# A two-layer diffusion step in float32: the opening reads its first scale columns in two chunks, and sums all shift columns on TensorE

## The chip, the cores and the metric

The kernel runs on one core of a Trainium2 chip. The metric is the device time of one execution in microseconds. A change of under about 0.3% (4 us) can't be told from none with a few runs of this kernel.

## The reference, cut to what matters

128 context tokens and 512 latent tokens of width 1024 go through two layers. Every layer has a mixer and a feed-forward part, each behind a normalisation that is scaled and shifted by a modulation vector, and each added to x through a gate:

```
m = silu(cond) @ w_ada[l] + b_ada[l]          # 6 parts of 1024: shift, scale, gate, shift, scale, gate
h = rms_norm(x, g) * (1 + scale) + shift
x = x + gate * mixer(h)                        # layer 0: p = h @ w_in (1024 -> 2048), pooling and short conv, w_out
x = x + gate * swiglu(rms_norm(x, g2) * (1 + scale2) + shift2)
```

There are two condition vectors, one for the context tokens and one for the latents. So each part of m is a matrix of 1024 x 2 values, and each needs 4 MB of w_ada. For the first projection of layer 0 only the scale and, later, the shift are needed at once; everything else of m comes later.

## The kernel before, in words

x is held transposed, as 8 blocks of 128 features by 640 tokens (block k is features 128k to 128k+127). Each matmul operand is split into a high and a low float32r part, and a product of a weight block with an operand block takes three matmuls (high by high, high by low, low by high), each in two halves of 320 tokens. So one output block m takes 8 steps k of 6 matmuls. The first projection (win, 16 output blocks of 128) is called pi in the profile; two output blocks come from one 1 MB tile of weights, and each is split (`Stream.split`, `pair`, line 141) by a copy on ACT (line 144) and a subtraction on DVE (line 145).

**Scale into the operand, the rest afterwards.** `prep` (line 480) multiplies block k of x by its scale column (ACT, line 485) and forms the low part (DVE, line 487). The normalisation's factor per token is applied to the product (`scaled_main`, line 521, on DVE). The shift goes through the weights on its own: `first_bias` and `first_turn` (lines 870 to 889) for output blocks 0 to 2, and two extra columns of the operand for blocks 3 and on.

**Modulation columns, two ways.** On TensorE: `ada_load` (line 762) reads a chunk of 512 columns of w_ada (four blocks) as four DMAs of 512 KB, `ada_pe` (line 298) multiplies it by silu(cond), `ada_row` (line 322) copies the result to SBUF on ACT, `ada_turn` (line 327) turns it into columns with small matmuls, and `ada_done` (line 391) adds the bias on DVE and, for scales, makes the factor 1 + scale. On DVE: `AdaDve.run` (line 357) multiplies one block's transposed weights (a "row", one DMA of 512 KB) by the silu'd condition vectors `silb`, in two instructions of line 372, one for each condition. Both kinds of DMA land in the same six buffers (tag `araw`), so a later load waits until an earlier buffer was read.

**Order of the opening.** Lines 768 to 904 stand in a manual schedule: every engine runs them in the order written. All DMAs are issued on one queue, SP's, in order. The order on SP is scale chunk 2 (4 DMAs), constants, x blocks 0 to 3, weight tile 0 (in two halves), scale chunk 3, x blocks 4 to 7, `silb`, two rows, shift chunk 0, weight tile 1, two rows, `pwr`, weight tile 2. While data are awaited, TensorE runs filler matmuls (`turn_over`, line 812). Scale chunk 2 then gives scale blocks 0 to 3; `prep` runs for these; output blocks 0 and 1 are computed for k 0 to 3; chunk 3 gives the other scale blocks, and the same follows for k 4 to 7. `silb` gets its silu on ACT at line 843, beside that. Of the shift, blocks 0 to 3 come over TensorE and blocks 4 to 7 as four rows on DVE (lines 848 to 855). Output block 2 and the norm's second half follow, then the shifts of the three first output blocks, and the splits for block 3 (`ws.split(3)`, line 893) and block 4 (`ws.split(4)`, line 903).

**After the opening.** `project` (line 556) runs output blocks 3 to 15 of pi. For each it takes the split weights, runs `ada.run` for one or two rows (line 1053), issues the 48 matmuls, and calls `mixer_in` (line 1028). For blocks 0 to 3 that is the pooling branch (`pool_branch`, line 920: copies on ACT at line 926, sums on DVE at line 933; `pool_mid`, line 939, and `pool_end`, line 956, some blocks later), for the others the convolution. Here the order within an engine is the scheduler's, near the order of the program, with a row pinned behind the DVE instruction traced before it (line 383). PSUM has three large buffers, which pi's output blocks and the four products `py` of `pool_end` take in turn: 3, 4, 5, py 0, 6, py 1, and so on. So output block 6 takes the buffer of block 4, and can't begin until block 4 has been scaled out of it (line 523 on DVE, line 528 on ACT).

Of the kernel before, what the change touches and what calls it, by code (L numbers as in the profile page):

```python
# [9 lines left out]
F32 = mybir.dt.float32  # L10
# [26 lines left out]
EARLY = 28  # L37
# [23 lines left out]
def hybrid_step(  # L61
# [9 lines left out]
    wada0,  # L71
    wada,
# [407 lines left out]
    def prep(k, dst, l, n):  # L480
        assert (l, 3 * n + 1, 4 if (l, 3 * n + 1, 4) in known and k < 4 else 8) in known
# [273 lines left out]
    with tc.tile_pool(name="pool1", bufs=1) as p1:  # L755
# [6 lines left out]
        def ada_load(ch):  # L762
            for q in range(4):
                raw = p0.tile([P, 2, 512], F32, tag="araw", bufs=6, name=f"raw_ada{ch}_{q}")
                nc.sync.dma_start(raw, wada0[(ch + 1) // 2 if ch < 3 else 2, q])
                ada_raw.append(raw)
# [4 lines left out]
            [(0, 4, 4)]  # L771
            + [(0, 8 * p, 8) for p in (2, 4, 3)]
# [5 lines left out]
        ada_load(2)  # L778
        nc.sync.dma_start(kc, konst)
        nc.sync.dma_start(x[:, 0:4, :], xT[:, 0:4, :])  # L780
        ws.load(1, cut=True)
        ada_load(3)
        nc.sync.dma_start(x[:, 4:8, :], xT[:, 4:8, :])

        nc.sync.dma_start(silb, crows[None].broadcast_to((P, 2, D)))
        ada.load()
        ada.load()
        ada_load(0)
        ws.load(2, cut=True)
        ada.load()  # L790
        ada.load()
        pwr = p0.tile([P, 512], F32, tag="pwr", name="pwr").rearrange("p (g c) -> p g c", g=4)
        nc.sync.dma_start(pwr, pw)
        ws.load(3)
        zero = p0.tile([P, 512], F32, tag="junk", name="zero")
# [21 lines left out]
        turn_over(6)  # L817
        acc = {ch: ada_acc(ch) for ch in (2, 3)}
        ada_pe(2, acc[2], range(4))
        row = ada_row(2, acc[2])  # L820
        turn_over(3)
        ada_turn(2, row)
        turn_over(14)
        for k in range(4):
            prep(k, bufA, 0, 0)
            if k == 1:
                ws.split(0, ahead=False)
        ws.split(1, ahead=False)
        for k in range(4):
            nrm.square(k)  # L830
        first_mm(0, range(4))
        ada_pe(3, acc[3], range(4))
        row = ada_row(3, acc[3])
        nrm.add_square(V)
        nrm.add_square(V)
        nrm.add_square(V)
        nrm.add_square(V)
        first_mm(1, range(2))
        ada_turn(3, row)
        first_mm(1, range(2, 4))  # L840
        for k in range(4, 8):
            prep(k, bufA, 0, 0)
        S.activation(silb, silb, AF.Silu)
# [4 lines left out]
        ada.run(1, hold=False)  # L848
        nrm.add_square(V)
        nrm.add_square(V)  # L850
        nrm.add_square(V)
        nrm.add_square(V)
        ada.run(1, hold=False)
        ws.split(2, ahead=False)
        ada.run(2, hold=False)
# [783 lines left out]
```

## Time and profile before

| | us |
|---|---|
| median of 3 runs | 1356.52 (1354.65 to 1358.49) |
| the profiled execution | 1359.17 |
| its span in the profile | 1357.0 |

The profile is of one execution. Its span runs from the first to the last instruction, and some 2.2 us of the execution's time lie around it. PE is TensorE, DVE VectorE, ACT ScalarE, SP the engine that issues the DMAs. Starts are in us from the beginning of the span. PE's granted clock is 1.00 where it runs at 2.4 GHz and 0.50 at 1.2 GHz.

### The profile page before, as it was taken

The page shows a single profiled execution, that of the slowest core. Times are in us where ns is not written, and L with a number is a line of the kernel's source. Part 1 is how long each engine was busy: PE and PEld are TensorE (multiplying, and loading weights), DVE is VectorE, ACT ScalarE, POOL GpSimd, SP SyncE. Part 2 cuts the span into 40 slices and gives each one's busy share as a digit, 9 for nine tenths or more (in the row PEclk, how much of TensorE's full clock was granted, in tenths as well). Part 3 has the DMA queues.
Part 4 walks back from the last instruction along what each step waited for, and adds up shares of the span by engine and source line. Part 5 has one row for each costly group of instructions (what it writes and reads, how often), then busy time and mean ns, then how long its engine had stood idle before and what let it go on. Part 6 is the DMA issues. An engine that isn't in the chain of part 4 may idle for free.

```text
span 1357.0 us, 22469 instructions
## 1 busy us (share of the span) xinstructions
PE 1327.6 (98%) x8952; PEld 1295.8 (95%) x8952; DVE 1076.8 (79%) x2095; ACT 638.5 (47%) x1159; POOL 46.3 (3%) x56
## 2 busy tenths in 40 slices
PE   9999999999999999999999999999999999999996
PEld 6899999999999999999998999999999999999995
DVE  4899897978999999999877677599877777446744
ACT  5433245753145521554666675477541355314543
POOL 0000000000000000000012221000000000000001
PEclk9899999999999999999999999999999999999998
DMA  9735422115433454344431110141144122311212
GB/s 366 284 109 190 168 94 94 63 63 171 171 124 111 156 189 151 124 135 161 148 101 48 48 48 32 34 154 47 47 140 164 39 94 70 118 63 63 78 47 78
DMA packets 36808, 155.54 MB, mean 115 GB/s; under 512 B 3936, under 2 KB 11104, under 8 KB 25952
## 3 DMA queue, kind: packets, MB, share of 16 engines
q1 hardware_dynamic: 36704, 154.12, 32.8%
q8 instruction: 70, 1.15, 0.3%
q14 instruction: 34, 0.28, 0.1%
HBM read 148.60 MB, written 2.88 MB: 112 GB/s over the span
## 4 chain that ended last, share of the span: by engine, by line
PE 82%; DVE 11%; ACT 3%; issue 2%; DMA 1%; SPq 0%; POOL 0%; DVEq 0%; ACTq 0%; POOLq 0%
PE fi L632 28%; PE fo L289 19%; PE fi L289 8%; PE pi L289 7%; PE pq L289 5%; PE po L289 4%; DVE junk L372 3%; PE wb L289 2%; PE wa L289 2%; PE o L1355 2%; PE s L1305 2%; DVE wl_fi_p L145 1%; PE t L1338 1%; ACT wh_fi_p L144 1%; DMA x<-xT 1%
## 5 line engine op out<-in xcount | busy, mean ns | idle before, releaser
L144 ACT ACTIVATE wh_fi_p<-raw_fi 128x512 fp32r<-128x512 f32 x252 | 154.5, 626 | 232.0 <-PE fi L632 123.6
L372 DVE CUSTOM_DVE_ANT_0 junk<-rawa,silb 128x512 f32<-128x512 f32 (+1 forms) x280 | 224.1, 800 | 5.9 <-DMA rawa<-wada 1.7
L145 DVE TENSOR_TENSOR wl_fi_p<-raw_fi,wh_fi_p 128x512 fp32r<-128x512 f32 x252 | 171.4, 687 | 65.0 <-ACT wh_fi_p L144 65.0
L144 ACT ACTIVATE wh_fo<-raw_fo 128x1024 fp32r<-128x1024 f32 (+1 forms) x48 | 47.5, 990 | 147.4 <-PE fo L289 122.8
L508 DVE SCALAR_TENSOR_TENSOR x<-fo,mod,x 128x128 f32<-128x128 f32 (+1 forms) x144 | 55.8, 434 | 70.4 <-PE fo L289 67.2
L632 PE MATMUL fi<-bh,wh_fi_p 128*128 128x320 f32 x288 | 88.8, 308 | 1.8 <-DVE x L508 1.8
L632 PE MATMUL fi<-bh,wl_fi_p 128*128 128x320 f32 x288 | 88.9, 309 | 0.0
L632 PE MATMUL fi<-ah,wl_fi_p 128*128 128x320 f32 x288 | 88.7, 308 | 0.0
L632 PE MATMUL fi<-al,wh_fi_p 128*128 128x320 f32 x288 | 88.7, 308 | 0.0
L632 PE MATMUL fi<-ah,wh_fi_p 128*128 128x320 f32 x288 | 88.5, 307 | 0.0
L632 PE MATMUL fi<-bl,wh_fi_p 128*128 128x320 f32 x288 | 88.4, 307 | 0.0
L289 PE MATMUL fo<-al,wh_fo 128*128 128x320 f32 x352 | 80.8, 310 | 0.0
L289 PE MATMUL fo<-ah,wh_fo 128*128 128x320 f32 x352 | 80.6, 310 | 0.1
L289 PE MATMUL fo<-ah,wl_fo 128*128 128x320 f32 x352 | 80.4, 309 | 0.0
L289 PE MATMUL fo<-bh,wh_fo 128*128 128x320 f32 x328 | 75.2, 310 | 0.0
L289 PE MATMUL fo<-bh,wl_fo 128*128 128x320 f32 x328 | 75.0, 310 | 0.0
L289 PE MATMUL fo<-bl,wh_fo 128*128 128x320 f32 x328 | 74.9, 310 | 0.0
L632 PE MATMUL fi<-x0h,wh_fi_p 128*128 128x320 f32 x216 | 68.1, 320 | 1.5 <-ACT fi L644 0.9
L632 PE MATMUL fi<-xh,wh_fi_p 128*128 128x320 f32 x216 | 67.9, 320 | 0.2
L632 PE MATMUL fi<-xh,wl_fi_p 128*128 128x320 f32 x216 | 66.5, 309 | 0.0
L632 PE MATMUL fi<-xl,wh_fi_p 128*128 128x320 f32 x216 | 66.5, 309 | 0.0
L632 PE MATMUL fi<-x0h,wl_fi_p 128*128 128x320 f32 x216 | 66.4, 308 | 0.0
(372 smaller groups left out, 3786.7 us busy)
## 6 DMA issues: line engine op xcount, KB each, us to landing
raw_fi<-wfi SPq DMA_DIRECT2D x44, 1024.0 KB, 4.7
rawa<-wada SPq DMA_DIRECT2D x84, 512.0 KB, 3.4
raw_fo<-wfo SPq DMA_DIRECT2D x16, 1024.0 KB, 4.9
raw_ada<-wada SPq DMA_DIRECT2D x12, 512.0 KB, 7.3
raw_in<-win SPq DMA_DIRECT2D x6, 1024.0 KB, 5.3
raw_fo<-wfo SPq DMA_DIRECT2D x8, 768.0 KB, 4.2
raw_qkv<-wqkv SPq DMA_DIRECT2D x6, 1024.0 KB, 5.4
raw_out<-wout SPq DMA_DIRECT2D x4, 1024.0 KB, 5.2
```

Source lines behind the costliest of these rows:

```text
L144: S.activation(h, src, AF.Copy)
L145: eng.tensor_tensor(out=l, in0=src, in1=h.bitcast(F32), op=ALU.subtract)
L289: PE.matmul(ps[:, h, 0 : hi - lo], w[a][:, k, cols], rhs[b][:, k0 + k, lo:hi], start=k == 0 and a == b, stop=k == kn - 1 and a == 1,)
L372: op = V.tensor_tensor_reduce(out=self.junk, in0=raw[:, cols], in1=self.silb[:, c, cols], scale=1.0, scalar=0.0, op0=ALU.mult, op1=ALU.add ...
L508: V.scalar_tensor_tensor(out=xs, in0=got[:, 0 : b - a], scalar=mod[l][:, gate0 + m, c : c + 1], in1=xs, op0=ALU.mult, op1=ALU.add,)
L632: PE.matmul(out, w[a][:, k, :], ops.get(OPERAND[p], b)[:, k, :], start=fresh and k == 0 and a == b, stop=k == ops.kn - 1 and a == 1, skip_ ...
L1305: PE.matmul(self.ps[:, hf, 0:HT], bufB[a][:, self.h, q0 : q0 + P], kt[b][:, self.kv, hf * HT : hf * HT + HT], start=n == 0, stop=n == 2,)
L1338: PE.transpose(flat(pt)[:, s * P : s * P + P], self.pe[:, s * P : s * P + P], ident)
L1355: PE.matmul(po[:, 0 : 2 * P], vt[a][:, self.kv, s * P : s * P + P], got[b][:, s, :], start=s == 0 and n == 0, stop=s == 4 and n == 2,)
```

## The change

Scale blocks 0 to 3 are read as two chunks of 256 columns (two blocks each, 1 MB in two DMAs), and x blocks 0 to 3 as two DMAs of two blocks. The new function `ada_half` sums one such chunk on TensorE, and `ada_half_turn` turns it. The first two output blocks start with k 0 and 1; the second half chunk and k 2 and 3 follow. The shift's blocks 4 to 7 become chunk 1 on TensorE, so the four early rows on DVE go. On SP weight tile 1 and both shift chunks now stand ahead of `silb`. The silu of `silb` moves to the end of the opening, between the last `first_turn` and the split for block 4, and two rows on DVE follow that split. The rows of the output blocks 3 to 15 are given by a list, 14 in all where 16 were. Output block 2's steps are spread anew between the shift's sums. The array of rows shrinks by the four blocks that are no longer rows, and the array of chunks changes accordingly. The diff leaves out a new argument, a looser assertion in `prep`, and one index of the last rows (76 becomes 72).

```diff
@@ -34,7 +34,9 @@
 PLAIN = 4
 RAW = 3
 
-EARLY = 28
+EARLY = 24
+
+PI_ROWS = (1, 0, 0, 1, 0, 1, 2, 1, 2, 1, 2, 1, 2)
...
@@ -762,36 +765,42 @@
         def ada_load(ch):
             for q in range(4):
                 raw = p0.tile([P, 2, 512], F32, tag="araw", bufs=6, name=f"raw_ada{ch}_{q}")
-                nc.sync.dma_start(raw, wada0[(ch + 1) // 2 if ch < 3 else 2, q])
+                nc.sync.dma_start(raw, wada0[min(ch, 2), q])
+                ada_raw.append(raw)
+
+        def ada_load_half(half):
+            for q in range(2):
+                raw = p0.tile([P, 4, 256], F32, tag="araw", bufs=6, name=f"raw_adah{half}_{q}")
+                nc.sync.dma_start(raw, wadah[half, q])
                 ada_raw.append(raw)
 
         startup = ExitStack()
         startup.enter_context(tc.manual_schedule())
         ada = AdaDve(
-            [(0, 4, 4)]
-            + [(0, 8 * p, 8) for p in (2, 4, 3)]
+            [(0, 8 * p, 8) for p in (2, 4, 3)]
             + [(0, 40 + b, 1) for b in range(8)]
             + [(1, 8 * p, 8) for p in (1, 0, 2, 4, 3)]
         )
         ada.home(p0, p1, 6, junk, silb)
         ada.limit = EARLY
-        ada_load(2)
+        pwr = p0.tile([P, 512], F32, tag="pwr", name="pwr").rearrange("p (g c) -> p g c", g=4)
+        ada_load_half(0)
         nc.sync.dma_start(kc, konst)
-        nc.sync.dma_start(x[:, 0:4, :], xT[:, 0:4, :])
+        nc.sync.dma_start(x[:, 0:2, :], xT[:, 0:2, :])
         ws.load(1, cut=True)
+        ada_load_half(1)
+        nc.sync.dma_start(x[:, 2:4, :], xT[:, 2:4, :])
         ada_load(3)
         nc.sync.dma_start(x[:, 4:8, :], xT[:, 4:8, :])
+        ws.load(2, cut=True)
+        ada_load(0)
+        ada_load(1)
 
         nc.sync.dma_start(silb, crows[None].broadcast_to((P, 2, D)))
-        ada.load()
-        ada.load()
-        ada_load(0)
-        ws.load(2, cut=True)
-        ada.load()
-        ada.load()
-        pwr = p0.tile([P, 512], F32, tag="pwr", name="pwr").rearrange("p (g c) -> p g c", g=4)
         nc.sync.dma_start(pwr, pw)
         ws.load(3)
+        for _ in range(4):
+            ada.load()
         zero = p0.tile([P, 512], F32, tag="junk", name="zero")
         G.memset(zero, 0.0)
         zeror2 = p0.tile([P, 512], F32R, tag="zero", name="zeror")
@@ -814,53 +823,88 @@
             for _ in range(n):
                 PE.matmul(idle, zeror, zeror2, start=True, stop=True)
 
-        turn_over(6)
-        acc = {ch: ada_acc(ch) for ch in (2, 3)}
-        ada_pe(2, acc[2], range(4))
-        row = ada_row(2, acc[2])
+        half_acc = ada_acc("h")
+
+        def ada_half(half):
+            out = half_acc[:, 256 * half : 256 * half + 256]
+            for q in range(2):
+                raw = ada_raw.pop(0)
+                for j in range(4):
+                    PE.matmul(
+                        out[32 * j : 32 * j + 2, :],
+                        silc[:, 4 * q + j, :],
+                        raw[:, j, :],
+                        start=False,
+                        stop=q == 1,
+                        tile_position=(0, 32 * j),
+                        skip_group_check=True,
+                    )
+            row = tmp(f"rowh_{half}")[0:98, 0:256]
+            S.activation(row, out[0:98, :], AF.Copy)
+            return row
+
+        def ada_half_turn(half, row):
+            ps = ps_small(f"adath_{half}")
+            for b in range(2):
+                PE.matmul(
+                    ps[:, 2 * b : 2 * b + 2],
+                    row[:, b * P : b * P + P],
+                    kc[0:98, C_SUM : C_SUM + 2],
+                    start=True,
+                    stop=True,
+                )
+            ada_done(0, 8 + 2 * half, ps[:, 0:4].rearrange("p (b c) -> p b c", c=2))
+
+        turn_over(4)
+        row = ada_half(0)
         turn_over(3)
-        ada_turn(2, row)
-        turn_over(14)
-        for k in range(4):
+        ada_half_turn(0, row)
+        turn_over(10)
+        for k in range(2):
             prep(k, bufA, 0, 0)
-            if k == 1:
+            if k == 0:
                 ws.split(0, ahead=False)
         ws.split(1, ahead=False)
+        first_mm(0, range(2))
+        row = ada_half(1)
+        first_mm(1, range(1))
+        ada_half_turn(1, row)
+        first_mm(1, range(1, 2))
+        for k in range(2, 4):
+            prep(k, bufA, 0, 0)
         for k in range(4):
             nrm.square(k)
-        first_mm(0, range(4))
-        ada_pe(3, acc[3], range(4))
-        row = ada_row(3, acc[3])
-        nrm.add_square(V)
-        nrm.add_square(V)
-        nrm.add_square(V)
-        nrm.add_square(V)
-        first_mm(1, range(2))
+        first_mm(0, range(2, 4))
+        acc = ada_acc(3)
+        ada_pe(3, acc, range(4))
+        row = ada_row(3, acc)
+        for _ in range(4):
+            nrm.add_square(V)
+        first_mm(1, range(2, 4))
         ada_turn(3, row)
-        first_mm(1, range(2, 4))
         for k in range(4, 8):
             prep(k, bufA, 0, 0)
-        S.activation(silb, silb, AF.Silu)
+        ws.split(2, ahead=False)
         for k in range(4, 8):
             nrm.square(k)
         first_mm(0, range(4, 8))
         first_mm(1, range(4, 8))
-        ada.run(1, hold=False)
-        nrm.add_square(V)
-        nrm.add_square(V)
-        nrm.add_square(V)
-        nrm.add_square(V)
-        ada.run(1, hold=False)
-        ws.split(2, ahead=False)
-        ada.run(2, hold=False)
-        S.preload_act_table_set("natural_log_exp_and_others")
+        for _ in range(4):
+            nrm.add_square(V)
+        first_mm(2, range(0, 2))
         acc = ada_acc(0)
         ada_pe(0, acc, range(4))
         row = ada_row(0, acc)
+        S.preload_act_table_set("natural_log_exp_and_others")
+        first_mm(2, range(2, 3))
+        ada_turn(0, row)
         nrm.finish((0, HT), None)
-        first_mm(2, range(0, 1))
-        ada_turn(0, row)
-        first_mm(2, range(1, 5))
+        first_mm(2, range(3, 4))
+        acc = ada_acc(1)
+        ada_pe(1, acc, range(4))
+        row = ada_row(1, acc)
+        first_mm(2, range(4, 5))
+        ada_turn(1, row)
         prep_shift(bufA, 0, 0)
         for b, t in enumerate(bufA):
             V.tensor_copy(shr[:, :, 2 * b : 2 * b + 2], t[:, :, T:TX].bitcast(F32))
@@ -888,11 +932,11 @@
             PE.matmul(pb[:, 0:2], row, kc[0:4, C_SEL : C_SEL + 2], start=True, stop=True)
             S.activation(fev[m][:, T:TX], pb[:, 0:2], AF.Copy)
 
-        first_mm(2, range(5, 6))
+        first_mm(2, range(5, 7))
         row = first_bias(0)
         ws.split(3, ahead=False)
         fev.append(scaled_main(first[1], "ev_1"))
-        first_mm(2, range(6, 8))
+        first_mm(2, range(7, 8))
         fev.append(scaled_main(first[2], "ev_2"))
         pwp = tuple(t[:, KB - 1, 0:512].rearrange("p (g c) -> p g c", g=4) for t in bufB)
         pair(pwp, pwr)
@@ -900,7 +944,9 @@
         rows = [first_bias(m) for m in (1, 2)]
         for m in (1, 2):
             first_turn(m, rows[m - 1])
+        S.activation(silb, silb, AF.Silu)
         ws.split(4, ahead=False)
+        ada.run(2, hold=False)
         startup.close()
 
 
@@ -1050,7 +1096,7 @@
             13,
             lambda i, ps: mixer_in(i + 3, scaled(ps, f"ev_{i + 3}")),
             ext=True,
-            each=lambda i: ada.run(1 + (5 <= i < 8)),
+            each=lambda i: ada.run(PI_ROWS[i]),
         )
 
...
@@ -1614,7 +1659,8 @@
         "rope": _rope(),
         "ckT": i["cache_k"][0, 0].transpose(2, 1, 0),
         "cv": i["cache_v"][0, 0],
-        "wada0": i["w_ada"][0].reshape(4, 2, P, 12, 512)[:, :, :, [0, 2, 3]].transpose(3, 0, 2, 1, 4),
+        "wada0": i["w_ada"][0].reshape(4, 2, P, 12, 512)[:, :, :, [0, 1, 3]].transpose(3, 0, 2, 1, 4),
+        "wadah": i["w_ada"][0][:, D : D + 512].reshape(2, 4, P, 2, 256).transpose(3, 0, 2, 1, 4),
         "wada": i["w_ada"].transpose(0, 2, 1).reshape(96, P, D)[_ADA_ORDER],
         "win": _tiles(_blocks(i["w_in_even"][0], _IN_ORDER)),
         "pw": i["pool_w"][0].transpose(1, 0, 2),
```

## Rows read from the trace of the kernel before

**Rows 1.** The page's first part: busy us of each engine (share of the span) xinstructions.

```profile
PE 1327.6 (98%) x8952; PEld 1295.8 (95%) x8952; DVE 1076.8 (79%) x2095; ACT 638.5 (47%) x1159; POOL 46.3 (3%) x56
```

**Rows 2.** Windows: stretch, its length, then busy us of each engine, granted clock, DMA share, GB/s.

```profile
5.00:10.00 5.00, 4.47 (x18) 0.37 (x16) 0.00 (x0) 0.00 (x0) 0.00 (x0) 1.00 1.05 417
...
37.00:41.00 4.00, 1.89 (x9) 0.98 (x7) 3.91 (x7) 3.12 (x4) 0.00 (x0) 0.98 1.04 386
41.00:47.50 6.50, 6.50 (x26) 6.50 (x27) 6.29 (x13) 1.18 (x3) 0.00 (x0) 0.50 1.01 408
...
58.00:80.60 22.60, 20.79 (x140) 20.52 (x139) 22.60 (x40) 10.39 (x16) 0.51 (x9) 1.00 0.36 128
81.00:90.00 9.00, 9.00 (x51) 9.00 (x52) 9.00 (x17) 2.33 (x5) 0.16 (x3) 0.81 0.49 177
90.00:150.00 60.00, 60.00 (x406) 60.00 (x405) 57.30 (x89) 18.96 (x30) 0.33 (x6) 1.00 0.50 170
```

**Rows 3.** The chain of waits, opening: start us, length us, engine, what it writes, line.

```profile
3.76 8.99 DMA x<-xT
...
53.47 2.01 PE fbias L875 x32
...
80.93 8.93 PE pi L289 x48
...
90.74 7.15 PE pi L289 x48
```

**Rows 4.** The timeline of PE: start us, length, line, form; in brackets idle before and its releaser.

```profile
9.24 1.03 PE L306 MATMUL adap<-raw_ada,silc 128*2 128x512 f32 x4 [0.26 <-DMA raw_ada<-wada]
...
20.19 2.32 PE L306 MATMUL adap<-raw_ada,silc 128*2 128x512 f32 x16
...
24.31 0.95 PE L330 MATMUL adat<-kc,row 98*128 98x2 f32 x8
...
34.57 0.40 PE L319 MATMUL adap<-zeror 128*128 128x512 f32 x1
...
37.45 0.78 PE L466 MATMUL ms_a<-ssq_a,ones 128*128 128x320 f32 x2 [0.28 <-DVE ssq_a L430]
38.97 0.55 PE L289 MATMUL pi<-ah,wh_in 128*128 128x320 f32 x2 [0.74 <-ACT wh_in L144]
...
40.90 0.90 PE L289 MATMUL pi<-ah,wl_in 128*128 128x320 f32 x2 [1.09 <-DVE wl_in L145]
...
55.72 0.57 PE L289 MATMUL pi<-ah,wh_in 128*128 128x320 f32 x2
...
80.93 0.56 PE L289 MATMUL pi<-ah,wh_in 128*128 128x320 f32 x2 [2.14 <-ACT ev L528]
```

**Rows 5.** The timeline of ACT, same columns.

```profile
25.70 3.74 ACT L485 ACTIVATE ah<-x,sc 128x128 fp32r<-128x128 f32 x8 [2.54 <-DVE sc L403]
29.34 1.90 ACT L843 ACTIVATE silb<-silb 128x2048 f32<-128x2048 f32 x1
...
37.85 1.06 ACT L144 ACTIVATE wh_in<-raw_in 128x1024 fp32r<-128x1024 f32 x1 [4.10 <-DMA raw_in<-win]
38.93 1.28 ACT L856 ACT_TABLE_LOAD   x1
40.22 0.60 ACT L324 ACTIVATE row<-adap 98x512 f32<-98x512 f32 x1
...
56.78 0.17 ACT L889 ACTIVATE ev<-fturn 128x2 f32<-128x2 f32 x1 [0.48 <-PE fturn L888]
56.85 1.05 ACT L144 ACTIVATE wh_in<-raw_in 128x1024 fp32r<-128x1024 f32 x1
```

**Rows 6.** The timeline of DVE, same columns.

```profile
57.94 1.23 DVE L145 TENSOR_TENSOR wl_in<-raw_in,wh_in 128x1024 fp32r<-128x1024 f32 x1 [1.39 <-ACT wh_in L144]
...
79.79 0.82 DVE L523 TENSOR_TENSOR ev<-pi,rstd 128x640 f32<-128x640 f32 x1
```

**Rows 7.** Windows of line 372 alone (the modulation rows): stretch, length, DVE busy, clock, DMA.

```profile
58.00:80.60 22.60, 6.20 (x11) 1.00 0.36 128
```

More of the change, by code (lines that the diff above doesn't have):

```diff
@@ L71, in hybrid_step @@
     wada0,
+    wadah,
     wada,
@@ L480, in prep @@
     def prep(k, dst, l, n):
-        assert (l, 3 * n + 1, 4 if (l, 3 * n + 1, 4) in known and k < 4 else 8) in known
+        assert any((l, 3 * n + 1, m) in known for m in range(k + 1, 9))
         h, lo = dst
@@ L1513, in hybrid_step @@
     S.activation(silb, silb, AF.Silu)
-    gates = AdaDve([(1, 40 + b, 1) for b in range(8)], 76)
+    gates = AdaDve([(1, 40 + b, 1) for b in range(8)], 72)
     gates.home(p3, p3, 2, ps_small("junk1"), silb)
@@ L1571 @@
 _FFN_ORDER = [b + j for j in range(FB) for b in (0, FB)]
-_ADA_ORDER = [4, 5, 6, 7]
-_ADA_ORDER += [8 * p + b for p in (2, 4, 3, 5, 7, 6, 8, 10, 9, 11) for b in range(8)]
+_ADA_ORDER = [8 * p + b for p in (2, 4, 3, 5, 7, 6, 8, 10, 9, 11) for b in range(8)]
 _SHAPES = (
```

## Prediction

> **What bounds the kernel now.** I read the page's first part, then the windows over the opening, then the chain of waits, and last the timelines of PE, ACT and DVE around each gap of PE. PE is busy for 1327.6 of 1357.0 us [rows 1], so from the end of the opening on the kernel takes as long as PE's work does, and what PE loses before that is lost for good. The reader is to see three losses. First, PE begins real work only when x has landed, at 3.76 + 8.99 = 12.75 us [rows 3]; until then the DMA queue is full, at 417 GB/s [rows 2]. Second, around 37 to 41 us PE is busy for 1.89 of 4.00 us: it waits 0.28 for the norm's sum, 0.74 for a weight split (ACT itself waited 4.10 us for that tile to land) and 1.09 for its low part [rows 2, 4, 5]; after this the granted clock is 0.50 for 6.5 us [rows 2], which costs half of that, 3.3 us. Third, output block 6 waits 2.14 us until 80.93 [rows 4]. This is a DVE queue: DVE is busy for all of 22.60 us from 58 [rows 2], and the instruction that frees the buffer, the scaling of output block 4, runs at 79.79 as the end of that queue [rows 6]. The clock then stands at 0.81 [rows 2]: block 6 takes 8.93 us where its neighbour takes 7.15 [rows 3], so 1.8 us more. From 90 to 150 us PE is never idle, and DVE is busy for 57.30 of 60 us [rows 2].
>
> **Step 1, the first scale in halves.** Ahead of the first operand the queue now carries 1.05 MB of scale columns less, and 0.66 MB of x less. These 1.70 MB at 417 GB/s are 4.1 us, so x blocks 0 and 1 land at about 8.7, and the first half tile of weights at about 10.2. The scale's sums end sooner by 1.05 MB, 2.5 us: they ended at 9.24 + 1.03 = 10.3 [rows 4], and will at 7.8; row copy, turn and factor follow as before, so `prep` starts at about 9.8 instead of 12.8. Gain at this point 3 us.
>
> **Step 2, the second half.** It needs 1.05 MB more and then x blocks 2 and 3. With the bytes laid end to end behind those of step 1 the second scale half lands at about 14, x at 15.6. Two steps k for blocks 0 and 1 cover part of that. Sums, row copy, turn and factor put `prep(2)` at 17.0. Behind it PE runs, in the written order, two steps of block 0, the sums of chunk 3 (0.4 for the zeros, 2.32 [rows 4]), two steps of block 1 and the turn (0.95 [rows 4]). A step of 6 matmuls is 7.15 / 8 = 0.89 us [rows 3]. That is 18.0 + 1.8 + 2.7 + 1.8 + 0.9 = 25.2, and the factor is there at 25.6. Before, `prep(4)` started at 25.70 [rows 5]: **the whole lead of step 1 is gone there**. What stays is that 1.8 us of block 1's work, before done behind the turn, is already done; the wait for `prep(4)` (1.0 us) takes half of it. Blocks 0 and 1 end at 25.6 + 1.0 + 8 x 0.89 = 33.7; before, the next sum began behind them at 34.57 [rows 4]. Gain 0.9 us.
>
> **Step 3, block 2 and the shifts.** PE then has 8 steps (7.1), two chunks summed and turned (2 x 3.6), two norm sums (0.78 each [rows 4]), 3.0 for the three biases (two took 2.01 [rows 3]) and some 0.9 for their turns: 19.6 us, so the last turn is copied at about 53.4. Before, the copy stood at 56.78 [rows 5]. The second chunk adds 3.6 us of PE work; the four rows, 10 us of DVE, go; the 2.1 us of waits and the 3.3 us of half clock go as well, if nothing takes their place: weight tile 1 now comes ahead of `silb` and both shift chunks, and lands at about 27.6, while its split follows `prep(7)` at 29.4. The last two DMAs of chunk 1 wait for buffers that the sums of chunk 0 free at about 36.5; landing some 4 us later they are still a microsecond ahead of PE. Everything on SP behind them (`silb`, `pwr`, tile 2, the rows) lands by 52, before it is used. Net gain at this point 3.4 us; bounds 0 (a clock drop, below) and 4.4 (if step 2's wait is nil).
>
> **Step 4, the silu moves behind this.** Before, the silu of `silb` (1.90 us) ran on ACT beside PE's work at 29.34, with the table it needed still loaded [rows 5]. Now it stands behind the norm's Ln and Exp, so a table load comes before it: 1.28 us, by the one at 38.93 [rows 5]. In ACT's queue the split for block 4 is behind both, and the low part on DVE behind that. So 53.5 + 1.28 + 1.90 + 1.05 puts the low part at 57.7, where it stood at 57.94 [rows 6]. DVE sits idle for 4 us meanwhile. **The gain of step 3 is spent here**, in full. The page "ScalarE: Activation LUTs" of the Trainium skill (section "What ACT_TABLE_LOAD costs") speaks against this move: a switch of tables costs, besides the load, a drain of about the same length. Here the row behind the load starts at 40.22, 0.01 us after it ends [rows 5], so I take 1.28 alone.
>
> **Step 5, DVE's queue up to block 4.** From the low part to the scaling of block 4 DVE had 22.66 us of work without a gap [rows 2, 6]. In it were two and a half rows: 6.20 us in eleven instructions, five of them halves of a row [rows 7]; a row is 2.5 us. After the change the two rows at the end of the opening stand at the head of that queue, and block 3's row behind them; blocks 4 and 5 have none. That is three rows: the queue gets longer by 1.3 us. Where block 4's row filled the time until the pooling's copy was made there is now a hole, about 1.0 us. So block 4 is scaled at 57.7 + 22.7 + 2.3 = 82.7, and block 6 starts at 83.0 instead of 80.93: **2.1 us later**. PE itself is there at 52.9 + 3 x 7.2 + 0.9 = 75.4, so its pause is about 7.5 us instead of 2.14.
>
> **Step 6, the clock behind that pause.** Before it cost 1.8 us behind 2.14 us [rows 3, 4], and 3.3 us behind the scattered 2.1 us at 37 to 41 [rows 2]. Between these bounds, 0 and 1.5 us over what block 6 paid before, I take the middle, 0.8.
>
> **Step 7, the rest.** Both kernels have 16 rows from 58 us to the end of pi, and 8 in the output projection; the later list has more at the end (8 against 5 in the last five blocks), covered by DVE's 2.7 us of idle time and by the first two blocks of the output projection, about 12 us of PE work that doesn't need the last of DVE's. If that cover were gone, 3 rows would cost at most 7.5 us. Behind pi nothing changes. DMAs: sixteen of 512 KB for the sums where twelve were, three for x where two were, four fewer for rows; the queue is full while they are issued, which hides them; without that cover a DMA takes its place on SP among the others, and a late one would show as a wait at step 2.
>
> **Sum.** 2.1 + 0.8 = +2.9 us, so 1359.17 would become 1362.1 in the profiled execution's terms. That one is 2.65 us over the median of 1356.52, hence 1359.4 in the median's.
>
> **The rivals.** *A, the pool work isn't held up.* The scheduler, not the program, orders what follows the opening. If it puts the three rows behind the scaling of block 4, that comes at 82.7 - 7.5 = 75.2, just when PE is ready. Then PE loses neither the 2.14 us nor the 1.8 us of half clock, and keeps its 2.8 us lead at block 3: 6.7 less; as DVE has only 2.7 us to spare up to 150 us, I count 6. That is 1350.5. For it speaks that rows are spread as filler now; against it that the two rows stand in the manual part, and DVE has nothing else ready there. *B, slower.* PE waits 1.5 us for `prep(4)`, right behind sums and turns. If this lowers the clock as the gaps at 37 to 41 did [rows 2, 4], the next 3.5 to 6.5 us run at 0.50, and blocks 0 and 1 end 1.7 to 3.3 us later. All behind it, ACT's and DVE's chain too, shifts by as much: +2.9 + 2.5 = 1361.9. It decides if that one pause does what the three at 37 to 41 did together. *C, ACT stands still at the table switch.* If it loses another load's length, 1.28 us [rows 5], ahead of the silu, the low part and all behind it come later: +4.2, 1360.7. The one switch in these rows shows nothing of the kind. The Trainium skill's page "ScalarE: Activation LUTs" (the section named above) states it as a drain. *D, nothing moves.* DVE's queue closes up the hole and the row: 1356.5.
>
> **How the numbers follow.** My forecast has 0.50, A 0.27, B 0.15, C 0.04, D 0.04. Over 0.3% (4.07 us) slower is above 1360.6: all of C and nearly all of B, and a third of the forecast, whose clock and scheduling terms can add 2 us. Faster by as much is below 1352.5: nearly all of A. So 0.25 faster, 0.40 the same, 0.35 slower. The range runs from A's 1350.5 to B's upper end (5.5 to 6.5 us) at 1363.
>
> **What would show it.** `prep` starts at 9 to 10.5, `prep(4)` within 1 us of 25.7, the last shift copy at 52.5 to 54.5, a table load and the silu right behind it, two rows at the head of DVE's queue, block 6 idle for 5 us or more before it, starting at 82 to 84.5. I am wrong if the scaling of block 4 ends before 79, if the three rows stand behind it, or if the clock in 25 to 50 us is not 1.00.

## The result and the profile after

| | before | after |
|---|---|---|
| median of 6 runs each | 1357.25 us (1354.65 to 1358.49) | 1362.24 us (1360.96 to 1362.98) |
| the profiled execution, its span | 1359.17 us, 1357.0 us | 1361.85 us, 1359.8 us |

The ratio is 1.0032, with a 95% interval of 1.0022 to 1.0042: the change costs 4.3 us by the ratio and 5.0 by the medians, where 2.9 were forecast. The spans differ by less, 2.8 us, because the profiled execution of before lay 1.9 us above its median and that of after 0.4 below. (Further down, one run of the variant with the split ahead of the silu took 2064.0 us at a mean granted clock of 0.58, and the ratios leave it out.) Where the loss arises is seen from the first feed-forward product `fi`: the view of that tile says when it started first and last. Before:

```profile
L632 PE MATMUL fi<-bh,wh_fi_p x288: 304/308/384, 271.2 to 613.1; 128*128 128x320 f32 x144
```

After:

```profile
L635 PE MATMUL fi<-bh,wh_fi_p x288: 304/308/386, 275.9 to 617.2; 128*128 128x320 f32 x144
```

It starts 4.7 us later than before, and nearly all of this has arisen by the output projection, which started at 156.59 us before and starts at 161.25 after, 4.66 later. The 1.9 us by which the spans differ less come behind this start, in part from 700 to 800 us, where PE was busy for 95.40 us before and for 96.72 after; they were not followed further. (Lines of the kernel after are 3 higher in the helpers and some 45 higher from the opening on.)

The page's first part and five windows of the kernel after (stretch, length, busy us of PE, PEld, DVE, ACT, POOL, granted clock, DMA share, GB/s):

```profile
PE 1328.0 (98%) x8987; PEld 1296.1 (95%) x8987; DVE 1068.7 (79%) x2081; ACT 640.8 (47%) x1162; POOL 46.9 (3%) x56
...
30.00:41.00 11.00, 10.99 (x76) 9.08 (x76) 7.17 (x11) 5.35 (x10) 0.00 (x0) 1.00 0.45 178
41.00:56.00 15.00, 15.00 (x132) 12.36 (x130) 7.34 (x17) 8.21 (x17) 0.35 (x6) 1.00 1.01 392
58.00:80.60 22.60, 19.71 (x132) 19.18 (x130) 19.94 (x34) 10.92 (x15) 0.35 (x6) 1.00 0.64 235
80.00:90.00 10.00, 7.21 (x30) 6.96 (x31) 10.00 (x18) 2.98 (x6) 0.17 (x3) 0.66 0.30 101
...
84.00:100.00 16.00, 16.00 (x91) 16.00 (x92) 12.10 (x20) 3.66 (x8) 0.33 (x6) 0.83 0.10 33
```

PE has nearly the same work as in [rows 1]. The waits and the half clock that before showed at 37 to 47.5 us [rows 2, 4] are gone: PE is busy throughout, at a clock of 1.00. But between 80 and 90 us PE is idle for 2.79 us, and from 84 to 100, where PE never waits, the clock is 0.83. In that last stretch 17% of 16 us is 2.7; before, 81 to 90 at 0.81 [rows 2] cost 1.7.

ACT after (start, length, line, form, wait and its releaser):

```profile
10.67 1.01 ACT L488 ACTIVATE ah<-x,sc 128x128 fp32r<-128x128 f32 x2 [2.21 <-DVE sc L406]
...
17.47 0.39 ACT L843 ACTIVATE rowh<-adap_h 98x256 f32<-98x256 f32 x1 [2.99 <-PE adap_h L833]
19.26 1.93 ACT L488 ACTIVATE ah<-x,sc 128x128 fp32r<-128x128 f32 x4 [1.40 <-DVE sc L406]
...
28.16 2.21 ACT L488 ACTIVATE ah<-x,sc 128x128 fp32r<-128x128 f32 x5 [2.50 <-DVE sc L406]
...
56.28 0.17 ACT L933 ACTIVATE ev<-fturn 128x2 f32<-128x2 f32 x1 [0.49 <-PE fturn L932]
56.47 1.28 ACT L947 ACT_TABLE_LOAD   x1
57.77 1.92 ACT L947 ACTIVATE silb<-silb 128x2048 f32<-128x2048 f32 x1
59.59 1.04 ACT L147 ACTIVATE wh_in<-raw_in 128x1024 fp32r<-128x1024 f32 x1
```

The first `prep` starts 2.2 us earlier than before, at 10.67. `prep(4)`, which started at 25.70 [rows 5], now starts at 28.16. The shifts still end 0.5 us earlier (56.28 for 56.78), and then the table load and the silu stand ahead of the split for block 4.

PE after:

```profile
16.36 1.04 PE L833 MATMUL adap_h<-raw_adah,silc 128*2 128x256 f32 x16
18.32 0.50 PE L849 MATMUL adath<-kc,rowh 98*128 98x2 f32 x4
...
26.77 0.95 PE L333 MATMUL adat<-kc,row 98*128 98x2 f32 x8
29.23 0.56 PE L292 MATMUL pi<-ah,wh_in 128*128 128x320 f32 x2 [1.50 <-ACT ah L488]
...
38.79 0.40 PE L322 MATMUL adap<-zeror 128*128 128x512 f32 x1
...
80.53 0.56 PE L1006 MATMUL py<-bh 128*128 128x320 f32 x2 [2.56 <-ACT ev L531]
83.95 0.90 PE L292 MATMUL pi<-ah,wh_in 128*128 128x320 f32 x2 [2.25 <-DVE bl L1015]
```

The row at 38.79 is the zeros of the next shift sum. They stand behind two steps of block 2, which took 1.77 us, so blocks 0 and 1 ended at 37.0; before, they ended at 34.57 [rows 4]. The opening's halves lose 2.4 us. Later, PE waits twice: 2.56 us ahead of `py_0`, whose buffer block 3 holds, and 2.25 us behind it. Before, `py_0` began without a wait, and there was one wait of 2.14 [rows 4]:

```profile
77.73 0.46 PE L960 MATMUL py<-bh 128*128 128x320 f32 x2
```

DVE after, from the low part for block 4 on (`junk` at line 375 is half a modulation row, `ev` at line 526 the scaling of a block, `bl<-py` frees the buffer of `py_0`):

```profile
60.66 1.23 DVE L148 TENSOR_TENSOR wl_in<-raw_in,wh_in 128x1024 fp32r<-128x1024 f32 x1 [4.37 <-ACT wh_in L147]
61.80 1.22 DVE L375 CUSTOM_DVE_ANT_0 junk<-rawa,silb 128x1024 f32<-128x1024 f32 x1
...
63.71 1.22 DVE L375 CUSTOM_DVE_ANT_0 junk<-rawa,silb 128x1024 f32<-128x1024 f32 x1
...
65.69 1.22 DVE L375 CUSTOM_DVE_ANT_0 junk<-rawa,silb 128x1024 f32<-128x1024 f32 x1
...
67.59 1.22 DVE L375 CUSTOM_DVE_ANT_0 junk<-rawa,silb 128x1024 f32<-128x1024 f32 x1
...
76.30 1.22 DVE L375 CUSTOM_DVE_ANT_0 junk<-rawa,silb 128x1024 f32<-128x1024 f32 x1
...
77.65 1.22 DVE L375 CUSTOM_DVE_ANT_0 junk<-rawa,silb 128x1024 f32<-128x1024 f32 x1
...
79.40 0.82 DVE L526 TENSOR_TENSOR ev<-pi,rstd 128x640 f32<-128x640 f32 x1
...
83.02 0.88 DVE L1015 SCALAR_TENSOR_TENSOR bl<-py,sm,bh 128x640 fp32r<-128x640 f32 x1
```

The `ev` at 79.40 is the scaling of block 3, not of block 4. Before, it stood at 70.90:

```profile
67.80 1.22 DVE L372 CUSTOM_DVE_ANT_0 junk<-rawa,silb 128x1024 f32<-128x1024 f32 x1
...
69.15 1.22 DVE L372 CUSTOM_DVE_ANT_0 junk<-rawa,silb 128x1024 f32<-128x1024 f32 x1
...
70.90 0.82 DVE L523 TENSOR_TENSOR ev<-pi,rstd 128x640 f32<-128x640 f32 x1
```

Six half rows lie ahead of it where before there were two. The four more, at 1.15 us each, are 4.6 us, and there is one more low part: together 5.8 us on top of a start 2.7 us later.

### The profile page after: what moved, and what is told of

Read it like the earlier page. It is cut to its first block, busy times and chain, and to the rows that moved or that the text cites. A ratio compares the mean times of both kernels' runs of the same rounds, so it can differ in the third digit from the quotient of the medians.

```text
span 1359.8 us, 22528 instructions
## 1 busy us (share of the span) xinstructions
PE 1328.0 (98%) x8987; PEld 1296.1 (95%) x8987; DVE 1068.7 (79%) x2081; ACT 640.8 (47%) x1162; POOL 46.9 (3%) x56
## 3 DMA queue, kind: packets, MB, share of 16 engines
q8 instruction: 70, 1.15, 0.3%
## 4 chain that ended last, share of the span: by engine, by line
PE 84%; DVE 11%; ACT 2%; issue 2%; DMA 0%; POOL 0%; DVEq 0%; SPq 0%; ACTq 0%; POOLq 0%
PE fi L635 28%; PE fo L292 19%; PE fi L292 8%; PE pi L292 7%; PE pq L292 5%; PE po L292 4%; DVE junk L375 3%; PE wb L292 2%; PE wa L292 2%; PE o L1401 2%; PE s L1351 2%; DVE wl_fi_p L148 1%; PE t L1384 1%; ACT wh_fi_p L147 1%; PE fo L1536 1%
## 5 line engine op out<-in xcount | busy, mean ns | idle before, releaser
L375 DVE CUSTOM_DVE_ANT_0 junk<-rawa,silb 128x512 f32<-128x512 f32 (+1 forms) x272 | 214.3, 788 | 3.1
L147 ACT ACTIVATE wh_fo<-raw_fo 128x1024 fp32r<-128x1024 f32 (+1 forms) x48 | 47.5, 990 | 147.1 <-PE fo L292 128.4
```

What stands on the lines that cost most here:

```text
L147: S.activation(h, src, AF.Copy)
L375: op = V.tensor_tensor_reduce(out=self.junk, in0=raw[:, cols], in1=self.silb[:, c, cols], scale=1.0, scalar=0.0, op0=ALU.mult, op1=ALU.add ...
```

## The experiments

Each ratio is to the kernel before in runs taken beside it. "fi" is the first start of that product in the profiled execution: 271.2 before and 275.9 after.

| run | median us | ratio (95%) | fi |
|---|---|---|---|
| after, split ahead of the silu | 1360.74 | 1.0020 (1.0010 to 1.0029) | 273.0 |
| after, silu early | 1359.28 | 1.0009 (0.9999 to 1.0018) | 271.7 |
| after, rows later | 1356.01 | 0.9989 (0.9980 to 0.9999) | 269.5 |
| after, 4 fillers | 1363.01 | 1.0042 (1.0025 to 1.0059) | 277.4 |
| after, chunk 2 whole | 1359.15 | 1.0019 (1.0009 to 1.0029) | 272.7 |
| before, rows later | 1360.16 | 1.0023 (1.0012 to 1.0033) | 270.9 |
| after, silu early and rows later | 1359.37 | 1.0015 (1.0005 to 1.0024) | 272.7 |
| after, whole, early, later | 1356.80 | 0.9999 (0.9990 to 1.0009) | 270.3 |
| after, whole and rows later | 1353.93 | 0.9977 (0.9968 to 0.9986) | 267.9 |
| after, second sums first | 1362.18 | 1.0040 (1.0027 to 1.0052) | 276.4 |
| after, PE reordered | 1359.33 | 1.0010 (1.0001 to 1.0019) | 274.0 |
| after, PE reordered, rows later | 1354.01 | 0.9969 (0.9958 to 0.9980) | 268.8 |

The runs were taken in several sessions, and the median of the kernel before lay between 1357.0 and 1358.2 us in them. So a gain that is read below as a difference from the 1362.24 of after is good to about 1 us. By the ratios the early silu brings 3.1 us, the later rows 5.8, the whole chunk 1.8 and the reordered PE 3.0.

**Steps 4 and 5: the silu and the rows.** First, the split for block 4 ahead of the silu:

```diff
+        ws.split(4, ahead=False)
         S.activation(silb, silb, AF.Silu)
-        ws.split(4, ahead=False)
         ada.run(2, hold=False)
```

> The changed kernel with the silu of silb placed behind the split for block 4 instead of ahead of it. My theory (the loss is ACT's and DVE's queue behind the last shift turn): the low part for block 4 moves from 60.66 to about 57.5 us, but the two rows behind it still wait for the silu, which then ends at about 60.6, so DVE's queue shifts by only 1.1 us; the time falls by about 1.1 us, to 1361.1. Rival (the loss is TensorE's extra sums and the slow start of the opening): no change, 1362.2, because PE is not touched.

Second, the silu where its table was still loaded (between the squares of blocks 4 to 7 and the copy of chunk 0's row), with `silb` read ahead of chunk 0:

```diff
+        nc.sync.dma_start(silb, crows[None].broadcast_to((P, 2, D)))
         ada_load(0)
...
         first_mm(2, range(0, 2))
+        S.activation(silb, silb, AF.Silu)
         acc = ada_acc(0)
...
-        S.activation(silb, silb, AF.Silu)
```

> The changed kernel with silb loaded ahead of the two shift chunks, and its silu on ACT between the squares and the copy of shift chunk 0, where the silu's table is still loaded. My theory: table load and silu (3.2 us) leave the path, the low part for block 4 stands at about 57.4, PE goes on at about 80.7 instead of 83.95 and pauses less; the time falls by 3.2 to 4 us, to 1358.5 to 1359. Rival: the loads of the shift chunks come 2.5 us later and PE waits for them, the time stays at 1362 or rises.

Third, no rows at the opening's end, and those two later, beside output blocks 7 and 10:

```diff
-PI_ROWS = (1, 0, 0, 1, 0, 1, 2, 1, 2, 1, 2, 1, 2)
+PI_ROWS = (1, 0, 0, 1, 1, 1, 2, 2, 2, 1, 2, 1, 2)
...
-        ada.run(2, hold=False)
         startup.close()
```

> The changed kernel without the two rows at the end of the opening; they are done beside output blocks 7 and 11 instead. My theory: DVE's queue ahead of the buffer that PE waits for is shorter by 4 halves of a row, 5 us; PE goes on at about 79 instead of 83.95, and with next to no pause the half clock behind it goes too (2.6 us); the time falls by 5 to 7.5 us, to 1355 to 1357, so under the kernel before. Rival (rows are only filler): the queue ends when it did, no change, or the rows come back as a wait in the last blocks, plus 2 us.

DVE with the split ahead of the silu, then with the silu early:

```profile
56.82 1.23 DVE L148 TENSOR_TENSOR wl_in<-raw_in,wh_in 128x1024 fp32r<-128x1024 f32 x1 [1.14 <-ACT wh_in L147]
60.05 1.23 DVE L375 CUSTOM_DVE_ANT_0 junk<-rawa,silb 128x1024 f32<-128x1024 f32 x1 [2.00 <-ACT silb L948]
```

```profile
57.04 1.23 DVE L148 TENSOR_TENSOR wl_in<-raw_in,wh_in 128x1024 fp32r<-128x1024 f32 x1 [1.14 <-ACT wh_in L147]
58.18 1.22 DVE L375 CUSTOM_DVE_ANT_0 junk<-rawa,silb 128x1024 f32<-128x1024 f32 x1
```

In the first the low part comes 3.8 us earlier, but the rows at the head of the queue then wait 2.00 us for the silu, and 1.5 us of the loss come back. In the second neither waits, and 3.0 us come back, near the 3.2 of table load and silu in step 4. The third, DVE with the rows later:

```profile
71.01 1.22 DVE L375 CUSTOM_DVE_ANT_0 junk<-rawa,silb 128x1024 f32<-128x1024 f32 x1
...
74.11 0.82 DVE L526 TENSOR_TENSOR ev<-pi,rstd 128x640 f32<-128x640 f32 x1
```

```profile
78.00:90.00 12.00, 9.97 (x68) 9.70 (x66) 12.00 (x22) 3.96 (x8) 0.33 (x6) 1.00 0.35 131
```

No row runs until 71.01, block 3 is scaled 5.3 us earlier, `py_0` doesn't wait (the wait behind it stays, 2.03 us), and the clock from 78 to 90 is 1.00 (0.72 after). The time falls by 6.2 us, below the kernel before. **The two rows at the head of DVE's queue are the largest single cost of the change.**

**Steps 1 and 2: the halves.** Fewer fillers:

```diff
-        turn_over(10)
+        turn_over(4)
```

> The changed kernel with 4 filler matmuls instead of 10 ahead of the first product. If the fillers at half clock hold up the first product (they end at 14.5 us, while its operands are there at 12.6 to 14.7), everything up to prep(4) comes 1.0 us earlier and the time falls by about 1 us, to 1361.2. If the fillers are what brings the clock up, the products after them run at half clock and the time rises by 1 to 3 us.

The first product began at 11.85 in place of 14.50, but each pair of matmuls took 0.73 to 0.90 us up to 15.5, where it takes 0.46 later. The second branch of the expectation names the cause: 0.73 is also what a pair took in the kernel before where the granted clock was 0.50 (43.84 to 47.04 us). `prep(4)` gained 0.4 us only (27.74), the clock fell behind the wait for it (0.90 from 24 to 41 us), and the time didn't fall (1363.01). Fewer fillers don't keep the lead. Now chunk 2 and x blocks 0 to 3 whole, with PE's order of the first 27 us as before and the rest as after (cut to its core):

```diff
-        ada_load_half(0)
+        ada_load(2)
...
-        nc.sync.dma_start(x[:, 0:2, :], xT[:, 0:2, :])
+        nc.sync.dma_start(x[:, 0:4, :], xT[:, 0:4, :])
...
-        row = ada_half(0)
+        ada_pe(2, acc[2], range(4))
+        row = ada_row(2, acc[2])
```

> The changed kernel with the first scale read and turned as one chunk, and x in two DMAs, as before the change; the shift sums, the silu's place and the rows stay changed. My theory now (the halves lose time: the products of blocks 0 and 1 begin 1.3 us sooner but end at 36.7 instead of 34.6 us): the last shift turn is copied about 2.1 us sooner than in the changed kernel, at 54.2, and the time falls by 2 us, to 1360.2. Rival, as I had predicted it (the halves gain 0.9 us): the time rises by 0.9 us, to 1363.1.

`prep(4)` then starts at 25.52, and the zeros that stood at 38.79 stand at 36.16: the halves cost 2.6 us there and, by the medians, 3.1 in all (1.8 by the ratio). Next, in the halved version, the second half's sums ahead of the first products:

```diff
-        turn_over(10)
+        turn_over(8)
...
-        first_mm(0, range(2))
         row = ada_half(1)
-        first_mm(1, range(1))
+        first_mm(0, range(1))
         ada_half_turn(1, row)
-        first_mm(1, range(1, 2))
+        first_mm(0, range(1, 2))
+        first_mm(1, range(2))
```

> The changed kernel with one edit in PE's written order: the second half's sums stand right behind the (eight) fillers and ahead of the first products, and its turn behind one step of block 0, where before it they stood behind two steps of block 0 and one of block 1. All of the reference is computed. Theory (the halves lose time because the second round of sums, copy, turn and factor stands behind the first products in PE's order, while its columns have landed at about 14): prep(2) starts at 17 to 17.8 in place of 19.26, prep(4) at 26 to 27 in place of 28.16, block 2's zeros 1.5 to 2 us ahead of 38.79, and the time falls by the same, to about 1360.3. Rival (the halves lose because chunk 3's columns and x blocks 4 to 7 land late, whatever PE's order): prep(2) earlier, prep(4) still at 28, and the time stays at 1362.

`prep(2)` (17.40) and `prep(4)` (26.79) came as expected, the gain didn't. PE, and the window behind it:

```profile
27.85 0.56 PE L292 MATMUL pi<-ah,wh_in 128*128 128x320 f32 x2 [1.51 <-ACT ah L488]
28.64 0.79 PE L292 MATMUL pi<-al,wh_in 128*128 128x320 f32 x2 [0.23 <-DVE al L490]
```

```profile
24.00:41.00 17.00, 15.27 (x97) 13.12 (x95) 8.65 (x15) 7.47 (x14) 0.00 (x0) 0.90 0.69 242
```

PE still waits 1.51 us, and this time it runs slower behind it: 0.74 us a pair until 31.9. Those 1.4 us give the gain back, and the zeros stand at 38.81. So the wait itself has to go. It is there because the changed order puts all four steps of block 1 ahead of chunk 3's turn; before, two stood behind it and covered `prep(4)`:

```diff
-        turn_over(10)
+        turn_over(8)
...
-        first_mm(0, range(2))
         row = ada_half(1)
-        first_mm(1, range(1))
+        first_mm(0, range(1))
         ada_half_turn(1, row)
-        first_mm(1, range(1, 2))
+        first_mm(0, range(1, 2))
+        first_mm(1, range(1))
...
-        first_mm(1, range(2, 4))
+        first_mm(1, range(1, 2))
         ada_turn(3, row)
+        first_mm(1, range(2, 4))
```

> The changed kernel, halves and all, with only PE's written order of the first 27 us altered: the second half's sums behind eight fillers and ahead of the first products, its turn behind one step of block 0, and the turn of chunk 3 ahead of block 1's steps for k 2 and 3, where the kernel before had it. All of the reference is computed. Theory (halves are no loss in themselves; what loses 2.6 us is that the second round and two more steps of block 1 stand ahead of chunk 3's turn, and nothing then covers the wait for prep(4)): prep(4) starts at 24.8 to 25.8, PE waits less than 0.5 us for it, block 2's zeros stand at 35 to 36 in place of 38.79, the pause behind block 5 is unchanged (two rows at the head of DVE's queue), and the time is 1358 to 1359.3. Rival (the waits at 13 to 15 us for the second half's columns lower the granted clock behind them, as in the run with that part alone): clock under 1.00 between 20 and 35 us, zeros at 37 or later, 1360 to 1362.

ACT and then PE of this run:

```profile
17.04 1.93 ACT L488 ACTIVATE ah<-x,sc 128x128 fp32r<-128x128 f32 x4 [1.40 <-DVE sc L406]
...
25.74 3.74 ACT L488 ACTIVATE ah<-x,sc 128x128 fp32r<-128x128 f32 x8 [2.29 <-DMA x<-xT]
```

```profile
26.81 0.56 PE L292 MATMUL pi<-ah,wh_in 128*128 128x320 f32 x2 [0.30 <-ACT ah L488]
...
36.37 0.40 PE L322 MATMUL adap<-zeror 128*128 128x512 f32 x1
```

The wait is down to 0.30 us, the clock is 1.00, and the zeros come at 36.37, 0.4 us later than was expected at the latest. The time falls by 2.9 us to 1359.33, at the edge of what was expected, and equals the version with the chunk whole. The reason it gains no more is in ACT's row: `prep(4)` now waits for x blocks 4 to 7, which land at 25.7, and so starts no sooner than with the chunk whole (25.52). Its factor was there at 25.05, so earlier blocks could have brought 0.7 us at most; this was not tried. **Halving the chunk gains nothing that can be told even in the mended order.**

**The parts together, and three misses.** The kernel before, with its rows later:

```diff
-            each=lambda i: ada.run(1 + (5 <= i < 8)),
+            each=lambda i: ada.run((1, 0, 0, 1, 1, 1, 2, 2, 2, 1, 2, 1, 2)[i]),
```

> The kernel before with the rows beside output blocks 3 to 15 spread as in the run a_late (1, 0, 0, 1, 1, 1, 2, 2, 2, 1, 2, 1, 2) instead of (1, 1, 1, 1, 1, 2, 2, 2, 1, 1, 1, 1, 1); nothing else. My theory: one half row less stands ahead of the scaling of block 4, so PE goes on about 1.2 us sooner, at 79.7; the pause shrinks to about 1 us, and with it the 1.8 us of half clock may go: 1.2 to 3 us less than before, 1354.5 to 1356.5. Rival (the rows' place is worth nothing without the rest of the change): 1357.7.

A miss: slower by 3 us, and not faster. DVE, then ACT:

```profile
76.85 1.22 DVE L145 TENSOR_TENSOR wl_in<-raw_in,wh_in 128x1024 fp32r<-128x1024 f32 x1 [0.42 <-ACT wh_in L144]
...
79.54 0.82 DVE L523 TENSOR_TENSOR ev<-pi,rstd 128x640 f32<-128x640 f32 x1
```

```profile
75.75 1.06 ACT L144 ACTIVATE wh_in<-raw_in 128x1024 fp32r<-128x1024 f32 x1 [4.34 <-PE pi L289]
```

With fewer rows, the scheduler put the split for block 8 (76.85) ahead of block 4's scaling, and that split waits on ACT until PE has done block 5 and set its weight buffer free (75.75). So block 4 is scaled at 79.54, as late as before (79.79), though this execution had come to the opening's end 1.9 us sooner, its clock from 41 to 47.5 us being 0.74 for 0.50. `fi` starts at 270.9, only 0.3 earlier. Its profiled execution is 1.4 us longer than that of before (spans 1358.4 and 1357.0), and what shows of this lies in the first feed-forward part. Two windows there of this kernel, then the same of the kernel before:

```profile
540.00:544.00 4.00, 3.15 (x15) 2.77 (x16) 4.00 (x10) 1.40 (x3) 0.00 (x0) 0.67 0.32 118
544.00:548.00 4.00, 4.00 (x17) 4.00 (x17) 3.83 (x11) 0.62 (x2) 0.00 (x0) 0.50 0.33 125
```

```profile
540.00:544.00 4.00, 2.79 (x17) 2.56 (x18) 4.00 (x11) 1.17 (x3) 0.00 (x0) 1.00 0.37 125
544.00:548.00 4.00, 4.00 (x30) 4.00 (x29) 4.00 (x12) 1.95 (x5) 0.00 (x0) 1.00 0.37 131
```

Both wait there twice, 1.86 and 0.83 us here, 1.81 and 0.95 before, and only here does the clock go to 0.50 (1.2 GHz), until 548 us. `fi` lasts until 615.4 for 613.1. That is 2.6 us more over `fi`, of which this execution gets a part back later. One execution doesn't say whether the others lose there as well, so what makes up the 3 us between the medians stays open.

The early silu and the later rows together, on the changed kernel, and then with the chunk whole as well:

> The runs a_early and a_late together. My theory: the low part for block 4 at about 57 us and no row behind it, so the scaling of block 4 ends at about 78.5 and PE pauses 1.5 us instead of 4.8; 1353 to 1354.5. Rival (a_late has already taken all there is to gain): 1356.

> b_whole, a_early and a_late together: the first scale as one chunk, the silu early, no rows at the head of DVE's queue. My theory: the gains add, the last shift turn at 54, the low part for block 4 at 55, PE goes on at 76.8 where it went on at 80.93 before; 1351 to 1352.5. Rival (from 90 us on DVE is full, so a lead of PE is given back as waits): no better than b_el.

Both missed by 4 to 5 us, and both show the order of the version of before with later rows: the split for block 8 stood ahead of block 4's scaling (at 76.17 and 78.86 in the second), block 6 followed `py_0`, and PE waited 3.77 us for that scaling. With the silu left late, block 7 takes `py_0`'s buffer instead and part of it runs ahead of block 6, so block 4's scaling isn't waited for. Hence the version with the chunk whole and the rows later, without the early silu:

> The changed kernel with two edits taken together: the scale chunk 2 and x blocks 0 to 3 whole again as in the kernel before, and no rows at the end of the opening with the later list (1,0,0,1,1,1,2,2,2,1,2,1,2). The silu stays at the opening's end. All of the reference is computed. Theory (the halves cost some 3 us of the opening, the two rows at the head of DVE's queue some 6 us of the wait behind block 5, and the two add because the second stage only waits for the first): 1362.2 - 3.1 - 6.2 = 1353, so 1352.5 to 1354; output block 7's steps stand ahead of block 6's as with the rows alone moved, block 4 is scaled at about 71.5 and the granted clock from 78 to 90 is 1.00. Rival (the earlier opening only meets the wait for the split of block 8, which stands behind PE's block 5, as in the run with all three edits): 1356 to 1357, and a pause of 2 us or more behind block 5.

1353.93 us, as the theory had it: **this beats both kernels**, by 3.1 and 8.3 us. Two things of the forecast failed: what is scaled at 71.04 is block 3 (block 4 follows at 80.80), and the clock from 78 to 90 is 0.86, behind a wait of 2.03 us. The same with the halves in the mended order:

> The same order of PE, and besides no rows at the end of the opening with the later list (1,0,0,1,1,1,2,2,2,1,2,1,2), as in the run with the rows alone moved. All of the reference is computed. Theory (the two parts add): about 3.5 us under that run's 1356.0, so 1352 to 1353.5, at or under the 1353.9 of the version with the whole scale chunk. Rival (the clock): 1355 to 1357.

1354.01 us, half a microsecond above the forecast and equal to the other within the spread, so the halves again neither help nor harm.

## Why the prediction was right and wrong

The direction, the range and the two causes at the opening's end held. The size didn't: 4.3 to 5.0 us for 2.9. Of the signs that it names, three failed (the first `prep`, `prep(4)` and the last shift copy came late), and those of the opening's end came. The sum's first half was wrong and its second half too pessimistic, and that the profiled execution came out at 1361.85 for the sum's 1362.1 is luck.

**Step 1** had the sign right: `prep` starts at 10.67, not at 9.8, a lead of 2.2 us and not 3. The three fillers between the sums and the turn took 1.58 us where the copy that they cover needs 0.38.

**Step 2 is the step that failed.** It put `prep(2)` at 17.0 from the bytes, as if sums could begin when the columns had landed. In the written order two steps of block 0, whose weights are split on ACT between the first `prep`s, stand ahead of these sums. They ran at 16.36, though the columns had landed by about 14.9 (there the run with the sums first waited last for them). `prep(2)` came at 19.26, 2.3 us late, and `prep(4)` at 28.16 for 25.6. I missed what stood ahead of `prep(2)`. Behind it the eight last steps took 7.8 us for 7.1, so blocks 0 and 1 ended 3.3 us later than the sum has it, and the gain of 0.9 was a loss of 2.4. Taking the halves out brought 3.1 us back (1.8 by the ratio), mending the order 2.9.

The order is not all of it, for the ten fillers ahead of the first products took longer in this execution than in another of the same code up to there. PE after, then PE and ACT with the rows later:

```profile
10.10 4.56 PE L824 MATMUL pi<-zeror 128*128 128x512 f32 x10
```

```profile
9.78 3.40 PE L824 MATMUL pi<-zeror 128*128 128x512 f32 x10
```

```profile
18.24 1.93 ACT L488 ACTIVATE ah<-x,sc 128x128 fp32r<-128x128 f32 x4 [1.40 <-DVE sc L406]
```

There `prep(2)` came at 18.24, so 1.0 of the 2.3 us is not the order but mostly the pace of the fillers, which the sum didn't price either (0.3 of it is a first `prep` that came sooner, at 10.35). That execution lost it again to the clock behind the wait for `prep(4)` (0.90 from 24 to 41 us): its zeros stand at 39.01, against 38.79.

**Step 3** held: from the end of blocks 0 and 1 to the last shift copy it gave 19.7 us (33.7 to 53.4); it took 19.3 (37.0 to 56.28), without a wait and at a clock of 1.00. Starting 3.3 us late, it ended 2.9 late.

**Step 4** held: copy to low part 4.2 us forecast, 4.38 measured. The silu starts at 57.77, 0.02 us after the load's end, so rival C did not happen. The Trainium skill's page "ScalarE: Activation LUTs" (section "What ACT_TABLE_LOAD costs") adds a drain of about 1.4 us to each switch; this trace doesn't show one on ACT's path.

**Step 5** had the cause (three rows where the wait begins) and the wrong place. I followed the queue to block 4's scaling and to block 6, at 25.3 us behind the low part. The rows fell ahead of block 3's scaling, since block 3 holds `py_0`'s buffer, and the scheduler put most of block 7 ahead of block 6, into that buffer: PE goes on at 83.95, when `py_0` has been read, while block 4 is scaled only at 89.15. PE took up `pi` again 23.3 us behind the low part, 2.0 less than forecast. With step 2's 2.9 us this gives 83.95 for 83.0: an error of 2.9 and one of -2.0 nearly hid each other. The experiments show both costs: some 6 us for the rows, 2 to 3 for the halves in this order.

**Step 6** said 0.8 more at half clock; 2.7 for 1.7 us is 1.0. **Step 7** said nothing elsewhere: 3.0 later at 83.95, 1.0 of clock and 0.2 for one wait at 102.08 are 4.2 of the 4.66 us by the output projection; where the other 0.4 arose is open.

Of the rivals, A failed since the two rows stayed at the head of the queue. Moved by hand, they brought 6.2 us against the kernel after, but only about 1.5 us against the kernel before (ratio 0.9989), where A had priced 6. B's fall behind the wait for `prep(4)` didn't occur in the profiled execution of the change, but in four of its variants it did, at 1.2 to 1.4 us instead of 2.5. D did not happen.

## What to carry to other kernels

When a load is cut in two so that work can start earlier, write down for the second half not when its bytes land but what stands ahead of its consumer in that engine's written order, and keep the old cover between a turn and the operand it makes. Follow a lengthened queue to the first buffer that it frees, not to the one that was waited for last time. Behind a manual schedule, judge an edit by the order that the scheduler then makes: taking work off an engine let a later split go ahead of the very instruction that was to come sooner.

## What was not expected of the hardware

- The same wait did not always have the same price. Seven kernels here keep the changed place of chunk 3's turn, and each waits 1.50 or 1.51 us for `prep(4)`. In the profiled executions of after, of the split ahead of the silu and of the early silu, the clock from 24 to 41 us is 1.00; with the rows later, where nothing in that stretch differs, it is 0.90, as with 4 fillers, with both silu and rows moved, and with the sums first. The two waits near 540 us are another such pair: 1.00 before, and 0.50 for a while in the version of before with later rows. A pause of PE is priced as a chance, not as a number. One thing goes with it in these executions: where the trace's first record of the clock at 1.00 begins at 13.6 to 14.5 us, as in the first three, it stayed; where it begins at 11.6 to 11.8 or, with 4 fillers, at 16.4, it fell. Why is not shown.
- Early in the run matmuls took long although the granted clock shows 1.00: the ten fillers behind the first turn took 4.56 us, 0.46 each, and the fourteen of before 3.44, 0.25 each. The column says nothing there: the trace's first record of the clock, at 1.00, begins at 14.5 us in the kernel after and at 6.7 in the one before, and ahead of the first record the view reads 1.00 for want of one. The fillers' times show the lower level until then. In the run with the rows later the record begins at 11.6, and the same ten fillers took 3.40 us.
